# HGRN2 head norm: both scaling multiplications issued one turn later, the first half's product in another tile

## The chip, the core and the metric

The kernel runs on one core of a Trainium2 chip. The metric is the device time of one execution in microseconds; three executions of the kernel before took 1461.38, 1464.78 and 1465.36 us (median 1464.78). A further execution was recorded by the hardware profiler. PE is the matrix engine (PEld its weight loads), DVE the vector engine, ACT the scalar engine, POOL the general engine GpSimd, SP the engine that here only issues DMAs.

## The reference, cut to what matters

The program is one layer of a hybrid trunk on x of 1 x 1024 x 1024: an input projection feeds three mixers (HGRN2 of four heads, attention over dilated windows, RWKV-7), whose outputs are concatenated and projected back; then a gated MLP, a gated embedding and a last norm. The change lies in the end of each HGRN2 head:

```python
_, o = lax.scan(step, s0, (chunks(q), chunks(k), chunks(i_raw.astype(f32)), chunks(log_f)))
o = o.transpose(1, 0, 3, 2, 4).reshape(B_, S_, HG_HEADS, HG_VDIM)
o = o * lax.rsqrt(jnp.mean(o * o, axis=-1, keepdims=True) + NORM_EPS)
o = o.reshape(B_, S_, HG_WIDTH) * gnorm_g.astype(f32) * jax.nn.silu(g_raw.astype(f32))
```

Per head o has 1024 positions x 128 values. Each position is divided by the root of the mean square of its 128 values, then multiplied by a weight and a gate.

## The kernel before, in words

The kernel works in f32 throughout; big matrix products are made of three passes over a split into high and low parts (L130, L132, L134). Its phases in order of time: the input norm and the first projections, RWKV with the other projections as filler, then from about 440 to 620 us the stretch in which the change lies (`phase_mix`, L317 to L328), then the output projection (`phase_out`), the MLP and the rest.

In the stretch four Python generators are issued in turns, and each `yield` ends a turn: A is HGRN2 head 0 and then head 2, B is head 1 and then head 3, C is the window attention (`swa`), F the last input projections (`project_late`, tiles named zp and zst). What a turn issues is not yet the order on the chip: a scheduler, which works with modelled times, places the instructions on each engine's queue when the program is built. The engines then run their queues in that order and wait for each other by semaphores. So moving a `yield` or a line changes the queues only where the scheduler's modelled times come out in another order.

A head (`hgrn_head`) works on positions laid along the 1024 columns of [128, 1024] tiles, which come from one pool of 11 slots (`self.slot`). It goes in these steps:

- f and q are loaded from DRAM (L984, L985, by SP; tile name zl). f is scaled (L987, DVE), k = 1 - f in two halves (L990, tile hk) and q*f (L992, 1024 wide, tile qt).
- Scores in eight levels: products (L1008, L1029, tile hsc), a masked copy into the score tile (L1010, L1031, tile hS), and updates of k (L1032, DVE or POOL in turn), of qt (L1034, DVE) and of the running products of f (L1039, tile hT). ACT copies the next level's keys (L1019, tile ks).
- Two masked copies close the scores (L1045, L1046).
- v is transposed (L1052) and copied to the tile hV (L1053), the keys likewise to hkt (L1058, L1059); the states are chained (L1073, L1080, L1082, tile hst).
- The output: for each half `hf`, PE makes four 128x128 blocks from hS and hV and from qt and hst (L1103, L1105); ACT copies them to the tile ho (L1106). `head_factor` makes the factor of the norm: squares on ACT into the old hkt (L1093), sum on DVE (L1094), mean and epsilon on DVE (L1095), power -1/2 on POOL (L1096, tile hrs). The half 0 uses the first half of hV, the half 1 the second.
- In the next turn the gate is loaded (L1110), the second half's factor is made and both halves of ho are multiplied by the factor, in place (L1114, DVE). After two more turns, of which one is empty, PE transposes the halves (L1121, tile vt), and DVE multiplies by weight and gate (L1122). The result is split for the output projection (`o_split`, `split_x`: ACT L155, then POOL or DVE L157; tiles xh, xl).

Other work that shares the queues here: the split of weights (L106 on ACT, L108 on POOL or DVE), the scaling of the last projections (L306, L475), the copies, sums and scaling of the attention (L1193 is one pass over logits, tile lg; L1210, tile pT; L1225 a small reciprocal; L1233, tile ob), and PE's attention products (L1186 tile swq, L1209 swt, L1222 swo, L189 swd). The PSUM pool mx, with four buffers, serves hsc, zp, vt, hkv, hpo, swt, swo and swd alike, so a late reader of one of these tiles holds up a PE product that needs the next buffer.

Of the kernel before, what the change touches and what calls it, by code (L numbers as in the profile page):

```python
# [14 lines left out]
ALU = mybir.AluOpType  # L15
# [3 lines left out]
P = 128  # L19
T = 1024  # L20
HT = 512
# [58 lines left out]
class Trunk:  # L80
# [896 lines left out]
    def hgrn_head(self, h):  # L977
        nc, mxp, par, spool = self.nc, self.mxp, self.par, self.spool
# [69 lines left out]
        V = self.slot("hV")  # L1048
        for hf in (0, 1):
            pt = mxp.tile([P, HT], F32, tag="mx", name=self.nm("vt"))  # L1050
# [4 lines left out]
        for hf in (0, 1):  # L1055
            pt = mxp.tile([P, HT], F32, tag="mx", name=self.nm("vt"))
# [30 lines left out]
        o3 = o.rearrange("p (c v) -> p c v", v=P)  # L1087
        sq3 = sq.rearrange("p (c v) -> p c v", v=P)
        ss, rs = (spool.tile([P, 8], F32, tag=n, name=self.nm(n)) for n in ("hss", "hrs"))

        def head_factor(hf):
            cs = slice(4 * hf, 4 * hf + 4)
            nc.scalar.activation(sq3[:, cs, :], o3[:, cs, :], AF.Square)  # L1093
            nc.vector.tensor_reduce(ss[:, cs], sq3[:, cs, :], AX.X, ALU.add)  # L1094
            nc.vector.tensor_scalar(ss[:, cs], ss[:, cs], 1.0 / P, EPS, ALU.mult, ALU.add)  # L1095
            nc.gpsimd.tensor_tensor(rs[:, cs], ss[:, cs], self.mhalf[:, :4], ALU.pow)  # L1096
# [12 lines left out]
        yield  # L1109
        oa = self.zload(j0 + 3, self.slot)  # L1110
        head_factor(1)
        for hf in (0, 1):
            oh = o3[:, 4 * hf:4 * hf + 4, :]
            nc.vector.tensor_tensor(oh, oh, rs[:, 4 * hf:4 * hf + 4].unsqueeze(2).broadcast_to([P, 4, P]), ALU.mult)  # L1114
        yield
        yield
        for hf in (0, 1):
            sl = slice((1 - hf) * HT, (2 - hf) * HT)
            pt = mxp.tile([P, HT], F32, tag="mx", name=self.nm("vt"))
            for c in range(4):  # L1120
                nc.tensor.transpose(pt[:, c * P:(c + 1) * P], o3[:, hf * 4 + c, :], self.ident)  # L1121
            nc.vector.scalar_tensor_tensor(oa[:, sl], pt if hf else pt[:, ::-1], par[:, PC_GN + h:PC_GN + h + 1], oa[:, sl], ALU.mult, ALU.mult)  # L1122
        self.o[h] = oa
        self.dump(f"o{h}", oa)
# [754 lines left out]
```

## Time and profile before

| what | value |
|---|---|
| median of three runs | 1464.78 us (1461.38 to 1465.36) |
| profiled execution, its own time | 1464.15 us |
| its span on the core (first to last instruction) | 1462.4 us |
| what lies around the span | 1.75 us |
| PE busy | 1431.1 us (98% of the span) |
| DVE busy | 1099.2 us (75%) |
| ACT, POOL busy | 636.1 us (44%), 447.8 us (31%) |
| granted TensorE clock, mean | 0.994 |
| stretch of the four heads, 490 to 620 us | PE busy 119.90 of 130 us, DVE 102.83 |

In a row of the timeline stand the start in us, the duration in us, the engine, the line, the operation, the tile written and the tiles read, their shapes and the count; in brackets the idle time of that engine just before the row and what ended it. Rows with a count above one are neighbours put together. In the table of windows a number stands beside each engine's busy time in brackets: the count of instructions. Idle time matters where it lies on the engine that the end of the program depends on.

### The profile page before, as it was taken

The numbers are of one execution on the slowest core, as the hardware profiler recorded it, in microseconds if no ns is written. First come the engines' busy times: TensorE is split into PE (matmuls) and PEld (weight loads), VectorE is DVE, ScalarE is ACT, GpSimd is POOL, SyncE is SP. The second block draws the span as 40 slices with busy tenths as digits, with TensorE's granted clock in tenths as the row PEclk, the third lists the DMA queues.
The fourth block names the chain that finished last, engine by engine and source line by source line (L and its number), as shares of the span: only waits on it lengthen the run. The fifth ranks groups of instructions, "written<-read, shape, count | busy, mean of one in ns | idle before, by whom it ended". The sixth has DMA issues, their size and how long they took to land.

```text
span 1462.4 us, 20341 instructions
## 1 busy us (share of the span) xinstructions
PE 1431.1 (98%) x7480; PEld 1178.0 (81%) x7480; DVE 1099.2 (75%) x1672; ACT 636.1 (44%) x1131; POOL 447.8 (31%) x364
## 2 busy tenths in 40 slices
PE   9999999999999999899989999999999999999996
PEld 7888887888877777788878888888888888888885
DVE  7667565674677688638778898888898799777685
ACT  6531443213434565335544344444444444455552
POOL 3331342223321131222144554444554000002342
PEclk9999999999999999999999999999999999999998
DMA  6123021240251320265423333333233883352343
GB/s 220 63 90 105 33 71 58 65 130 30 73 188 51 108 73 30 71 219 204 156 87 105 99 100 108 102 108 106 97 107 111 309 293 95 102 172 58 123 157 116
DMA packets 80020, 167.84 MB, mean 115 GB/s; under 512 B 20081, under 2 KB 22257, under 8 KB 79921
## 3 DMA queue, kind: packets, MB, share of 16 engines
q1 hardware_dynamic: 65568, 145.44, 30.2%
q10 hardware_dynamic: 13408, 17.57, 3.6%
q0 software_dynamic: 944, 3.54, 0.7%
q8 instruction: 59, 0.97, 0.3%
q14 instruction: 41, 0.33, 0.1%
HBM read 120.12 MB, written 46.40 MB: 114 GB/s over the span
## 4 chain that ended last, share of the span: by engine, by line
PE 87%; DVE 4%; issue 3%; ACT 2%; POOL 2%; DMA 2%; SPq 0%; DVEq 0%; ACTq 0%; POOLq 0%
PE bg L1351 16%; PE bv L1351 12%; PE dp L130 8%; PE dp L134 8%; PE dp L132 8%; PE bg L1652 7%; PE bv L1652 7%; PE hsc L1029 1%; PE bv L130 1%; PE bv L132 1%; PE bv L134 1%; PE bg L130 1%; PE bg L134 1%; PE bg L132 1%; PE swq L1186 1%
## 5 line engine op out<-in xcount | busy, mean ns | idle before, releaser
L130 PE MATMUL dp<-xh,whi 128*128 128x512 f32 x544 | 197.5, 408 | 0.8 <-ACT xh L375 0.8
L134 PE MATMUL dp<-xh,wlo 128*128 128x512 f32 x544 | 188.9, 392 | 0.3 <-POOL wlo L108 0.3
L132 PE MATMUL dp<-xl,whi 128*128 128x512 f32 x544 | 188.6, 392 | 0.0
L108 POOL TENSOR_TENSOR wlo<-raw,whi 128x512 fp32r<-128x512 f32 x84 | 138.0, 1662 | 80.9 <-ACT whi L106 80.9
L108 POOL TENSOR_TENSOR wlo<-wraw,whi 128x512 fp32r<-128x512 f32 x63 | 89.2, 1420 | 226.2 <-ACT whi L106 208.2
L1351 PE MATMUL bg<-t,whi 128*128 128x512 f32 x352 | 132.7, 389 | 0.0
L106 ACT CAST whi<-wraw 128x512 fp32r<-128x512 f32 x120 | 72.6, 617 | 129.1 <-PE dp L132 87.1
L130 PEld LDWEIGHTS dp<-xh,whi 128*128 128x128 f32 x544 | 101.6, 189 | 23.6 <-issue 3.5
L134 PEld LDWEIGHTS dp<-xh,wlo 128*128 128x128 f32 x544 | 102.3, 188 | 22.5 <-POOL wlo L108 0.7
L132 PEld LDWEIGHTS dp<-xl,whi 128*128 128x128 f32 x544 | 102.5, 189 | 20.2 <-DVE xl L376 0.5
L108 POOL TENSOR_TENSOR wlo<-s,whi 128x512 fp32r<-128x512 f32 x44 | 65.7, 1492 | 159.1 <-ACT whi L106 159.1
L106 ACT CAST whi<-raw 128x512 fp32r<-128x512 f32 x88 | 52.6, 619 | 100.3 <-PE bv L1351 51.5
L1652 PE MATMUL bg<-t,whi 128*128 128x512 f32 x308 | 94.9, 389 | 0.0
L1652 PE MATMUL bv<-t,whi 128*128 128x512 f32 x308 | 94.8, 389 | 0.0
L106 ACT CAST whi<-s 128x512 fp32r<-128x512 f32 x66 | 38.9, 620 | 120.7 <-PE bg L1351 113.0
L175 POOL TENSOR_TENSOR rst<-rst,mhalf 128x4 f32<-128x4 f32 (+1 forms) x9 | 10.2, 1130 | 222.7 <-DVE rst L173 222.7
L108 DVE TENSOR_TENSOR wlo<-wraw,whi 128x512 fp32r<-128x512 f32 x57 | 47.7, 837 | 40.2 <-ACT whi L106 35.8
L1351 PEld LDWEIGHTS bg<-t,whi 128*128 128x128 f32 x352 | 66.1, 188 | 13.7
L1648 ACT CAST t<-t 128x512 fp32r<-128x512 f32 x77 | 47.8, 622 | 47.9 <-PE bv L1652 33.0
L1652 PEld LDWEIGHTS bv<-t,whi 128*128 128x128 f32 x308 | 57.8, 188 | 12.0
L1652 PEld LDWEIGHTS bg<-t,whi 128*128 128x128 f32 x308 | 57.8, 188 | 11.9
L1351 PE MATMUL bg<-t,wlo 128*128 128x512 f32 x176 | 67.2, 389 | 0.0
(424 smaller groups left out, 3616.6 us busy)
## 6 DMA issues: line engine op xcount, KB each, us to landing
raw<-in_ffn_up_dram SPq DMA_DIRECT2D x44, 512.0 KB, 3.7
wraw<-in_w_in_dram SPq DMA_DIRECT2D x29, 512.0 KB, 3.7
z<-zst SPq DMA_DIRECT2D x18, 512.0 KB, 3.0
gb<-ct SPq DMA_DIRECT2D x33, 256.0 KB, 2.3
t<-gb SPq DMA_DIRECT2D x33, 256.0 KB, 2.8
t<-gt SPq DMA_DIRECT2D x33, 256.0 KB, 2.7
zl<-z SPq DMA_DIRECT2D x16, 512.0 KB, 4.5
wraw<-in_ple_gate_dram SPq DMA_DIRECT2D x16, 512.0 KB, 3.6
```

The costliest lines, as they stand in the source:

```text
L106: nc.scalar.copy(hi, src)
L108: eng.tensor_tensor(lo, src, hi.bitcast(F32), ALU.subtract)
L130: nc.tensor.matmul(ps[hf], wh, xh[hf], start=first, stop=False)
L132: nc.tensor.matmul(ps[hf], wh, xl[hf], start=False, stop=False)
L134: nc.tensor.matmul(ps[hf], wl, xh[hf], start=False, stop=last)
L175: nc.gpsimd.tensor_tensor(r2[:, :n], r[:, :n], self.mhalf[:, :n], ALU.pow)
L1029: nc.tensor.matmul(sc[:, c, :], ks[:, c * P:(c + 1) * P], view(qt, c * P, [2 * n, 64 // n], [HT + n, 2], [1, n]), start=True, stop=True)
L1186: nc.tensor.matmul(pq[h][:, b:b + w], d["q"][hs, qb * P:nk], d["k"][hs, b:b + w], start=True, stop=True)
L1351: nc.tensor.matmul(ps, w[part == 2][:, s], X[k][part == 1], start=start and k == part == 0, stop=k == 3 and part == 2, skip_group_check=no ...
L1648: nc.scalar.copy(xh, x)
L1652: nc.tensor.matmul(ps[m], wt[part == 2][:, m * P:(m + 1) * P], (xh, xl)[part == 1], start=k == part == 0, stop=k == NK - 1 and part == 2)
```

## The change

The two multiplications L1114 move behind one `yield`: they are issued one turn later, where before there was an empty turn. The first half's product is no longer written over ho but into the first half of hV, whose last reader in the program before was the half 0 of the output product. The transposes read the first half from there. The second half is still multiplied in place. The change adds no instruction that computes; hV stays in use until the transposes, and so does its slot.

```diff
@@ -1109,16 +1109,17 @@
         yield
         oa = self.zload(j0 + 3, self.slot)
         head_factor(1)
+        yield
+        normed = [V[:, :HT].rearrange("p (c v) -> p c v", v=P), o3[:, 4:, :]]
         for hf in (0, 1):
-            oh = o3[:, 4 * hf:4 * hf + 4, :]
-            nc.vector.tensor_tensor(oh, oh, rs[:, 4 * hf:4 * hf + 4].unsqueeze(2).broadcast_to([P, 4, P]), ALU.mult)
-        yield
+            cs = slice(4 * hf, 4 * hf + 4)
+            nc.vector.tensor_tensor(normed[hf], o3[:, cs, :], rs[:, cs].unsqueeze(2).broadcast_to([P, 4, P]), ALU.mult)
         yield
         for hf in (0, 1):
             sl = slice((1 - hf) * HT, (2 - hf) * HT)
             pt = mxp.tile([P, HT], F32, tag="mx", name=self.nm("vt"))
             for c in range(4):
-                nc.tensor.transpose(pt[:, c * P:(c + 1) * P], o3[:, hf * 4 + c, :], self.ident)
+                nc.tensor.transpose(pt[:, c * P:(c + 1) * P], normed[hf][:, c, :], self.ident)
             nc.vector.scalar_tensor_tensor(oa[:, sl], pt if hf else pt[:, ::-1], par[:, PC_GN + h:PC_GN + h + 1], oa[:, sl], ALU.mult, ALU.mult)
```

The lines behind it move by one: L1114 becomes L1116, L1122 becomes L1123, and so on.

In the queues the change moves nothing on POOL and SP, and a handful of rows on the others. Two places matter. The first is DVE at the end of head 0, where head 2 begins. The names: qt_4617 is head 2's q*f (L992); xl are splits for the output projection; zp and zst are a projection; hS and qt_3996 belong to head 1, zl_4446 is head 0's gate. Before:

```order
L992 TENSOR_TENSOR qt_4617<-zl_4550,zl_4548 128x1024
L157 TENSOR_TENSOR xl_4706<-ob_3827,xh_4705 128x512
L157 TENSOR_TENSOR xl_4710<-oc_1628,xh_4709 128x512
L306 TENSOR_TENSOR zp_4477<-zp_4477,rstd 128x512
L1031 COPY_PREDICATED hS_4036<-cmask,hsc_4506 128x512
L1034 TENSOR_TENSOR qt_3996<-qt_3996,hT_4038 128x2x8x32
L157 TENSOR_TENSOR xl_4712<-oc_3237,xh_4711 128x512
L1122 SCALAR_TENSOR_TENSOR zl_4446<-vt_4536,par,zl_4446 128x512
L475 TENSOR_TENSOR zst_4475<-zst_4475,zp_4477 128x512
L1122 SCALAR_TENSOR_TENSOR zl_4446<-vt_4542,par,zl_4446 128x512
L1031 COPY_PREDICATED hS_4036<-cmask,hsc_4552 128x512
L1034 TENSOR_TENSOR qt_3996<-qt_3996,hT_4038 128x2x4x64
```

And the end of the same piece with the change, which begins with the two L157 in the place of L992:

```order
L1123 SCALAR_TENSOR_TENSOR zl_4446<-vt_4542,par,zl_4446 128x512
L1031 COPY_PREDICATED hS_4036<-cmask,hsc_4552 128x512
L1034 TENSOR_TENSOR qt_3996<-qt_3996,hT_4038 128x2x4x64
L992 TENSOR_TENSOR qt_4617<-zl_4550,zl_4548 128x1024
L1045 COPY_PREDICATED hS_4036<-cmask,hS_4036 128x512
L157 TENSOR_TENSOR xl_4698<-zl_4446,xh_4697 128x512
```

L992 has moved behind eleven rows, to the place ahead of L1045. On SP the loads stand in the same order, but head 2's load of q now carries the wait that head 1's load of v, the next in the queue, had before, since the slots are given out otherwise.

The second place is DVE at the end of head 1. ho_4771, hss_4772 and hrs_4773 are head 1's; hS_4647 and hT_4649 are head 2's scores; zl_4907 is head 3's f; lg, swq and sden are the attention's. Before:

```order
L1193 ISA lg_4859,sden_4602<-swq_4853,swmask 128x512
L1193 ISA sden_4602 128x1
L1114 TENSOR_TENSOR ho_4771<-ho_4771,hrs_4773 128x512
L1031 COPY_PREDICATED hS_4647<-cmask,hsc_4841 128x512
L1034 TENSOR_TENSOR qt_4617<-qt_4617,hT_4649 128x2x64x4
L1032 TENSOR_TENSOR hk_4614<-hk_4614,hT_4649 128x2x32x8
L987 TENSOR_SCALAR zl_4907<-zl_4907,olb,lb 128x1024
L1225 RECIPROCAL sden_4602<-sden_4602 128x8
L1031 COPY_PREDICATED hS_4647<-cmask,hsc_4880 128x512
```

With the change:

```order
L1194 ISA lg_4859,sden_4602<-swq_4853,swmask 128x512
L1194 ISA sden_4602 128x1
L1031 COPY_PREDICATED hS_4647<-cmask,hsc_4839 128x512
L1034 TENSOR_TENSOR qt_4617<-qt_4617,hT_4649 128x2x64x4
L1116 TENSOR_TENSOR ho_4771<-ho_4771,hrs_4773 128x512
L1032 TENSOR_TENSOR hk_4614<-hk_4614,hT_4649 128x2x32x8
L1031 COPY_PREDICATED hS_4647<-cmask,hsc_4880 128x512
```

The second half's multiplication now stands behind one level's masked copy and its update of qt; L987 moves eleven rows down, ahead of its reader L990, with one L1032 between the two, and L1225 still further. On PE the same place had two attention products ahead of the score product hsc_4880 and now has one; the transposes follow the score product as before.

In the queues of heads 0, 2 and 3 the multiplications themselves stand where they stood.

## The prediction

> **What bounds the kernel now.** I read the page first: busy times, then the chain that ended last.
>
> ```profile
> span 1462.4 us, 20341 instructions
> PE 1431.1 (98%) x7480; PEld 1178.0 (81%) x7480; DVE 1099.2 (75%) x1672; ACT 636.1 (44%) x1131; POOL 447.8 (31%) x364
> ...
> PE 87%; DVE 4%; issue 3%; ACT 2%; POOL 2%; DMA 2%; SPq 0%; DVEq 0%; ACTq 0%; POOLq 0%
> ```
>
> PE is the bound: 1431.1 of 1462.4 us. An edit on DVE counts only where PE stands idle for DVE, or comes to. So I went to the windows around the two places where the queues differ (first number the width; then PE, PEld, DVE, ACT and POOL):
>
> ```profile
> 512.00:524.00 12.00, 11.79 (x101) 9.67 (x96) 11.77 (x16) 7.13 (x13) 5.38 (x4) 1.00 0.06 23
> 524.00:540.00 16.00, 16.00 (x112) 13.12 (x114) 11.87 (x34) 12.70 (x31) 6.01 (x6) 1.00 0.34 108
> 540.00:557.00 17.00, 14.46 (x112) 10.89 (x110) 16.44 (x32) 7.92 (x19) 3.84 (x5) 1.00 0.21 71
> ...
> 490.00:620.00 130.00, 119.90 (x945) 99.06 (x942) 102.83 (x196) 69.39 (x138) 33.64 (x30) 0.99 0.22 75
> ```
>
> From 512 to 524 us DVE is as full (11.77 of 12) as PE; from 524 to 540 PE never rests; from 540 to 557 DVE is full (16.44 of 17) and PE idles 2.54 us. What PE waits for in the whole stretch of the heads, 490 to 620 us (total, times, longest):
>
> ```profile
> PE hsc L1029 <- DVE qt L1034: 4.6, 4, 2.1
> PE vt L1121 <- DVE ho L1114: 1.5, 1, 1.5
> ```
>
> With some small ones it idles 10.1 us there (130 less 119.90), which caps any gain here. About 0.3% of this time, 4.4 us, is what a measurement can tell from no change; the cap is over that, the sums below are not.
>
> **The change part by part.** *The multiplications themselves.* There are eight, at 692 ns by the group's row, and eight after, with the same shape, so nothing is added to DVE's work.
>
> ```profile
> L1114 DVE TENSOR_TENSOR ho<-ho,hrs x8: 690/692/1533, 502.8 to 613.1; 128x512 f32<-128x512 f32 x8
> L1122 DVEq EVENT_SEMAPHORE  x4: 21/21/21, 511.8 to 613.1; - x4
> ```
>
> The first half's product into hV must also wait until PE has read hV. That wait is already over whenever the factor exists, since the factor is made from that product. What it costs is an added semaphore row on DVE: 0.02 us by the second row, three heads at most, 0.06 us; I take 0.05.
>
> *Head 2's q\*f (L992) eleven rows later.* The rows of DVE, with the ACT and POOL rows beside them:
>
> ```profile
> 507.69 0.80 DVE L987 TENSOR_SCALAR zl<-zl,olb,lb 128x1024 f32<-128x1024 f32 x1
> ...
> 509.20 1.22 DVE L992 TENSOR_TENSOR qt<-zl,zl 128x1024 f32<-128x1024 f32 x1
> ...
> 510.21 1.31 ACT L155 CAST xh<-oc 128x512 fp32r<-128x512 f32 x2 [0.74 <-PE zp L134]
> ...
> 510.94 0.68 DVE L157 TENSOR_TENSOR xl<-oc,xh 128x512 fp32r<-128x512 f32 x1
> ```
>
> Before, L992 filled a hole. The second xl behind it needs a cast on ACT that starts at 510.21, after a wait for PE, and two take 1.31 us, so it can't start before about 510.87 whatever DVE does. If L992 leaves, DVE stands idle for most of its 1.22 us and nothing behind comes earlier. Eleven rows on, it lands here:
>
> ```profile
> 516.82 0.67 DVE L1034 TENSOR_TENSOR qt<-qt,hT 128x512 f32<-128x512 f32 x1
> 517.23 1.41 POOL L157 TENSOR_TENSOR xl<-zl,xh 128x512 fp32r<-128x512 f32 x1 [10.01 <-ACT xh L155]
> ...
> 517.41 1.83 DVE L1045 COPY_PREDICATED hS<-cmask,hS 128x512 f32<-128x512 uint8 x1
> ...
> 519.06 1.30 POOL L108 TENSOR_TENSOR wlo<-wraw,whi 128x512 fp32r<-128x512 f32 x1 [0.42 <-ACT whi L106]
> ...
> 519.14 1.77 DVE L157 TENSOR_TENSOR xl<-zl,xh 128x512 fp32r<-128x512 f32 x1
> ...
> 568.03 0.72 DVE L1045 COPY_PREDICATED hS<-cmask,hS 128x512 f32<-128x512 uint8 x1
> ```
>
> L1045 alone takes 0.72 us (568.03); at 517.41 it took 1.83. POOL's row ended at 518.64, and L1045 at 519.24, 0.60 later: it stood still while POOL worked, and only then ran. The xl at 519.14 did the same behind POOL's L108 (520.36 to 520.91). So DVE's chain here is full and partly stalled, and it ends on PE:
>
> ```profile
> 523.13 0.67 DVE L1233 TENSOR_TENSOR ob<-ob,swd 128x512 f32<-128x512 f32 x1
> ...
> 523.95 1.06 PE L1058 MATMUL vt<-cst,hk 128*128 128x128 f32 x8 [0.21 <-DVE ob L1233]
> ```
>
> PE waits 0.21 us for L1233, which frees a PSUM buffer. There is no slack: what DVE loses between 517.4 and 523.8, PE loses at 523.95, and PE is full up to 540.
>
> With the change L992 starts at 517.41 and, having two inputs in SBUF like the xl, stands until POOL is done at 518.64; with its 1.14 (1.22 less the overlap of neighbouring rows) it ends about 519.78. Then come L1045 and the xl. If L1045 stands for POOL's L108 up to 520.4, it ends at 521.0; the xl is then free, and ends at 521.65, against 520.83 where the next row began before: +0.8 us. If the stalls stay as they are, the whole 1.14 comes on top. Bounds: nothing, where L992 isn't stalled and uses up the time in which L1045 stood; and +2.9, where each handover goes to POOL (rival 1). I take +1.0, nearest to the two rows that stalled.
>
> The Trainium skill ("SBUF — State Buffer", section "SBUF: two separate sides") says that an operation of DVE with two SBUF inputs and a GpSimd operation that reads SBUF exclude each other, and whoever starts first keeps the ports for the whole instruction. By that L992 would be held and would then hold POOL's L108. The two stalled rows agree with its first half; whether POOL then pushes back is rival 1.
>
> *The loads.* On SP, head 2's load of q takes over the wait that the next load in the queue had.
>
> ```profile
> 499.81 1.27 SPq L503 DMA_DIRECT2D zl<-z  x3
> ...
> DMA to landing us min/median/max: 3.1/4.2/5.9
> ```
>
> All three loads were issued within 1.27 us, so that wait was over by 500.66. At the longest landing, 5.9 us, q is there by 507, ten us before its new reader. Cost nil; without that cover, the delay of L992 would come on top.
>
> *Head 1's second half behind a masked copy and an update of qt.*
>
> ```profile
> 543.13 0.69 DVE L1193 CUSTOM_DVE_ANT_0 lg<-swq,swmask 128x512 f32<-128x512 f32 x1
> ...
> 544.34 0.69 DVE L1114 TENSOR_TENSOR ho<-ho,hrs 128x512 f32<-128x512 f32 x1 [0.52 <-POOL hrs L1096]
> 544.95 0.72 DVE L1031 COPY_PREDICATED hS<-cmask,hsc 128x512 f32<-128x512 uint8 x1
> 545.56 0.68 DVE L1034 TENSOR_TENSOR qt<-qt,hT 128x512 f32<-128x512 f32 x1
> ...
> 546.39 1.13 PE L1029 MATMUL hsc<-qt,ks 128*128 128x128 f32 x8 [0.72 <-DVE qt L1034]
> ...
> 554.04 1.13 PE L1029 MATMUL hsc<-qt,ks 128*128 128x128 f32 x8 [0.35 <-DVE qt L1034]
> 555.00 1.95 PE L1008 MATMUL hsc<-zl,hk 128*128 128x128 f32 x16
> ```
>
> DVE waited 0.52 us for the factor with a masked copy behind it whose product was long there. In the new order the copy starts at 543.8, qt is done about 545.0 instead of 546.2, and PE starts the score product about 545.1; one attention product now stands behind it, so nothing runs dry. PE wins most of the 0.72. The second wait, 0.35, goes too, as that product stands earlier. But the next one needs head 3's k:
>
> ```profile
> 553.81 0.76 DVE L990 TENSOR_SCALAR hk<-zl 128x512 f32<-128x512 f32 x2
> ```
>
> DVE's work up to the end of L990 (554.57) loses the wait of 0.52 and L1225 (0.12 as the rows step), and gains one L1032 that came later before (0.60): 554.53. So L1008 can start at 554.6 instead of 555.00: a gain of 0.4 us. That is what is late next. Bounds: 0, if POOL stalls another row here, and 0.72 + 0.35 = 1.07.
>
> *The other heads.* Heads 0, 2 and 3 keep their multiplications where they were. The last head shows what the edit might have shortened:
>
> ```profile
> 613.07 0.69 DVE L1114 TENSOR_TENSOR ho<-ho,hrs 128x512 f32<-128x512 f32 x1 [1.12 <-POOL hrs L1096]
> ...
> 613.91 1.06 PE L1121 MATMUL vt<-cst,ho 128*128 128x128 f32 x8 [1.54 <-DVE ho L1114]
> ```
>
> There the half 1 comes first on DVE and the half 0 last, and PE's queue has the half 0 first, before as after. So the 1.54 us stay.
>
> The sum: +1.0 - 0.4 + 0.05 = +0.65 us, on the profiled execution's own time of 1464.15 (span 1462.4 and 1.75 around): 1464.8 us. The median of the three runs is 1464.78, 0.6 over the profiled execution, and the lowest 1461.38, 2.8 under it; so this forecast is "no change".
>
> **The rivals.**
>
> *1. Slower: POOL and DVE hold each other up in turn.* Place: DVE and POOL from 517 to 526 us. L992 ends at 519.78, then POOL's L108 goes first (1.30, to 521.08), L1045 ends at 521.7, POOL's next split comes between again (1.5 us), and L1233 ends near 526.7 instead of 523.8: +2.9, less 0.4 and plus 0.05, gives 1466.7 us. It decides if POOL gets its turn at each of the two handovers. For it: POOL has four rows in 5.38 us of that window. Against it: the second of these splits waits for its own cast. Chance 0.2.
>
> *2. A little faster: L992 costs nothing.* If L992 runs beside POOL, and L1045 behind it is stalled less, the two rows take the time of the one. Then only -0.4 and 0.05 are left: 1463.8 us. For it: the L1034 at 516.82 kept its 0.67 us although POOL's row began before its end. Chance 0.2.
>
> *3. Faster: the last head's transposes no longer wait.* With the halves in two tiles, PE could start on one half while DVE works on the other; the 1.54 us of the last head would go: 1464.15 + 0.65 - 1.5 = 1463.3 us. Against: the queue has the late half first. Chance 0.05.
>
> *4. The change doesn't do what it says.* In three heads of four this is so already, since the scheduler had put the multiplications where their factor is ready. It is part of the forecast.
>
> **How the numbers follow.** The forecast has 0.5, rivals 1 to 3 have 0.2, 0.2 and 0.05; 0.05 is left for something that I don't see, such as shifted DMAs behind the stretch. All cases lie between 1463.3 and 1466.7 on the profiled execution; the three runs lay from 2.8 under to 1.2 over it, but their median varies less. I put 2 us below the lowest case and 0.3 above the highest: 1461.3 to 1467.0. The threshold of 4.4 us is reached by none of the cases, whether counted from 1464.15 or from the median. So: within 0.3% 0.92, faster by more 0.04 and slower by more 0.04, from the unseen rest and the spread of the runs.
>
> **What would show it right or wrong.** In the profile after: L992 near 517.4 with a duration over 1.22, idle DVE near 509.5, PE's L1058 about 1 us later with a wait of 1 us or more for DVE (under 0.3: rival 2; over 2: rival 1); near 545 the masked copy ahead of the multiplication and PE's wait there under 0.3; L1121 of the last head with its 1.5 us unchanged. I would be wrong if PE's idle time between 490 and 620 us changed by more than 3 us, or if the time moved with that idle time unchanged.

## The result, and the profile after

The kernel before took 1463.24 us (median of 8 runs, 1461.38 to 1465.36), the changed one 1467.93 us (8 runs, 1465.41 to 1469.87): ratio 1.0033, 95% interval 1.0023 to 1.0044, about +4.7 us, where +0.65 us and a time from 1461.3 to 1467.0 us were forecast. The profiled execution after took 1469.87 us (span 1468.1 and 1.8 around), 5.7 over the profiled one of before. The page after:

```profile
span 1468.1 us, 20345 instructions
PE 1433.5 (98%) x7480; PEld 1177.7 (80%) x7480; DVE 1101.9 (75%) x1672; ACT 636.3 (43%) x1131; POOL 448.2 (31%) x364
```

The same 7480 products keep PE busy 2.4 us longer, and the span has grown by 5.7. So both waits and the products themselves have to be looked at.

**End of head 0.** DVE, POOL and PE in the timeline after (start, duration; in brackets the idle time before and what ended it):

```profile
516.17 1.42 POOL L157 TENSOR_TENSOR xl<-zl,xh 128x512 fp32r<-128x512 f32 x1 [10.00 <-ACT xh L155]
516.37 2.31 DVE L992 TENSOR_TENSOR qt<-zl,zl 128x1024 f32<-128x1024 f32 x1
...
518.00 1.82 POOL L108 TENSOR_TENSOR wlo<-wraw,whi 128x512 fp32r<-128x512 f32 x1 [0.41 <-ACT whi L106]
...
518.60 1.83 DVE L1045 COPY_PREDICATED hS<-cmask,hS 128x512 f32<-128x512 uint8 x1
...
520.27 2.95 POOL L157 TENSOR_TENSOR xl<-oc,xh 128x512 fp32r<-128x512 f32 x2 [0.44 <-ACT xh L155]
520.32 1.77 DVE L157 TENSOR_TENSOR xl<-zl,xh 128x512 fp32r<-128x512 f32 x1
...
522.01 1.79 DVE L1046 COPY_PREDICATED hS<-cmask,few 128x512 f32<-128x512 uint8 x1
...
524.91 0.67 DVE L1234 TENSOR_TENSOR ob<-ob,swd 128x512 f32<-128x512 f32 x1
...
525.73 1.94 PE L1058 MATMUL vt<-cst,hk 128*128 128x128 f32 x8 [3.05 <-DVE ob L1234]
...
527.46 3.62 PE L1008 MATMUL hsc<-zl,hk 128*128 128x128 f32 x16
```

L992 takes 2.31 us in place of 1.22, and at every handover DVE and POOL stand for each other: L992 until POOL's split ends at 517.59, POOL's L108 until L992 ends at 518.68, L1045 until L108 ends at 519.82. PE's wait for L1234 has become 3.05 us (0.21 before). And then the products behind it are slow. In the windows after (width, busy time of PE, PEld, DVE, ACT and POOL, then the granted clock, 1.00 being full speed):

```profile
524.00:526.00 2.00, 0.27 (x2) 0.30 (x3) 2.00 (x4) 1.56 (x3) 0.00 (x0) 0.68 0.00 0
526.00:528.00 2.00, 2.00 (x11) 2.00 (x10) 0.60 (x5) 1.06 (x2) 0.00 (x0) 0.50 0.93 285
528.00:530.00 2.00, 2.00 (x11) 2.00 (x11) 0.59 (x1) 1.99 (x6) 0.00 (x0) 0.50 0.32 117
530.00:532.00 2.00, 2.00 (x14) 2.00 (x12) 0.89 (x2) 0.69 (x2) 0.84 (x1) 0.62 0.00 0
```

And PE's L1008 of before, with the clock at 1.00:

```profile
524.85 1.95 PE L1008 MATMUL hsc<-zl,hk 128*128 128x128 f32 x16
```

The clock is halved from about 524.7 to 531.5 us (by the shares of the first and the last window), and L1058 and L1008 take 1.94 and 3.62 us in place of 1.06 and 1.95. The same 122 products that follow from L1058 on (525.73 to 547.71 us, and 523.95 to 543.14 before) keep PE busy 20.59 us in place of 17.82. A wait of 3 us has cost PE nearly as much again.

**End of head 1.** DVE and PE after:

```profile
548.30 0.74 DVE L1031 COPY_PREDICATED hS<-cmask,hsc 128x512 f32<-128x512 uint8 x1
...
549.11 1.12 PE L1187 MATMUL swq<-zl,zl 64*128 64x512 f32 x2
549.52 0.68 DVE L1116 TENSOR_TENSOR ho<-ho,hrs 128x512 f32<-128x512 f32 x1
...
550.16 1.16 PE L1029 MATMUL hsc<-qt,ks 128*128 128x128 f32 x8
...
552.12 1.34 PE L1187 MATMUL swq<-zl,zl 64*128 64x512 f32 x6
...
555.24 1.22 DVE L157 TENSOR_TENSOR xl<-zl,xh 128x512 fp32r<-128x512 f32 x1
556.12 2.26 PE L1187 MATMUL swq<-zl,zl 64*128 64x512 f32 x4
556.38 0.81 DVE L1194 CUSTOM_DVE_ANT_0 lg<-swq,swmask 128x640 f32<-128x640 f32 x1
...
557.25 0.29 PEld L1187 LDWEIGHTS swq<-zl,zl 64*128 64x128 f32 x2 [0.84 <-DVE sden L1194]
```

The masked copy runs ahead of the multiplication, and PE's score product at 550.16 waits for nothing. But the attention products have changed. Before:

```profile
544.54 1.13 PE L1186 MATMUL swq<-zl,zl 64*128 64x512 f32 x4
...
548.33 0.49 PE L1186 MATMUL swq<-zl,zl 64*128 64x128 f32 x4
...
551.80 1.89 PE L1186 MATMUL swq<-zl,zl 64*128 64x512 f32 x8
```

Each uses 64 of PE's 128 rows. Two heads' products of 512 columns, one behind the other, took 1.13 us together (x4), and after, one alone takes 1.12 (x2): as a pair they run side by side. After, one pair is parted by the score product and the transposes (1.12 + 1.34 against 1.13 + 0.49), another by time: its second half must wait until the second logit pass (L1194) frees its buffer, and an xl of 1.22 us has come between the two passes (2.26, and 0.70 more for its 256 wide rest, against 1.89). This place of the xl is a third change in DVE's queue, beside the two shown ahead of the prediction: before, it stood behind both passes (551.99 us, 0.69 long).

**The sum.** From the transposes of head 0 to head 3's score product that waits longest for qt (595.00 before, 600.56 after): first all products, then the rows of the attention's tile swq alone (the products L1186 and L1187 with their weight loads and the DVE rows that read them; busy time of PE, PEld and DVE), of before:

```profile
513.58:595.00 81.42, 74.77 (x580) 59.67 (x579) 70.55 (x140) 47.29 (x101) 23.01 (x20) 1.00 0.16 53
```

```profile
513.58:595.00 81.42, 14.33 (x48) 5.47 (x48) 11.72 (x16) 1.00 0.16 53
```

and of after:

```profile
512.53:600.56 88.03, 79.34 (x580) 62.61 (x579) 74.02 (x141) 47.70 (x101) 24.70 (x20) 0.96 0.15 49
```

```profile
512.53:600.56 88.03, 16.24 (x48) 5.58 (x48) 11.76 (x16) 0.96 0.15 49
```

The stretch is 6.61 us longer. PE's idle time went from 6.65 to 8.69: 2.84 more at L1058, 0.80 less elsewhere, nearly all of it at the end of head 1 (1.25 to 0.46). Its busy time grew by 4.57: 1.91 in the attention products, the remaining 2.66 by the half clock (2.77 in the 122 products behind the wait, 0.11 less in overlaps elsewhere). The last head's transposes wait 1.45 us (1.54 before).

### The profile page after: what moved, and what is told of

Read it like the earlier page. It is cut to its first block, busy times and chain, and to the rows that moved or that the text cites. A ratio compares the mean times of both kernels' runs of the same rounds, so it can differ in the third digit from the quotient of the medians.

```text
span 1468.1 us, 20345 instructions
## 1 busy us (share of the span) xinstructions
PE 1433.5 (98%) x7480; PEld 1177.7 (80%) x7480; DVE 1101.9 (75%) x1672; ACT 636.3 (43%) x1131; POOL 448.2 (31%) x364
## 4 chain that ended last, share of the span: by engine, by line
PE 85%; DVE 5%; issue 3%; ACT 3%; POOL 1%; DMA 1%; SPq 0%; DVEq 0%; ACTq 0%; POOLq 0%
PE bg L1352 16%; PE bv L1352 12%; PE dp L130 7%; PE dp L134 7%; PE dp L132 7%; PE bg L1653 7%; PE bv L1653 7%; PE hsc L1029 2%; PE bv L130 1%; PE bv L134 1%; PE bv L132 1%; PE swq L1187 1%; PE bg L130 1%; PE bg L134 1%; PE bg L132 1%
## 5 line engine op out<-in xcount | busy, mean ns | idle before, releaser
L108 POOL TENSOR_TENSOR wlo<-raw,whi 128x512 fp32r<-128x512 f32 x84 | 138.0, 1662 | 80.8 <-ACT whi L106 80.8
L108 POOL TENSOR_TENSOR wlo<-wraw,whi 128x512 fp32r<-128x512 f32 x63 | 88.6, 1410 | 227.8 <-ACT whi L106 209.2
L108 POOL TENSOR_TENSOR wlo<-s,whi 128x512 fp32r<-128x512 f32 x44 | 65.4, 1487 | 159.4 <-ACT whi L106 159.4
L108 DVE TENSOR_TENSOR wlo<-wraw,whi 128x512 fp32r<-128x512 f32 x57 | 48.3, 847 | 40.1 <-ACT whi L106 35.7
```

The source lines that it names most:

```text
L108: eng.tensor_tensor(lo, src, hi.bitcast(F32), ALU.subtract)
```

## The experiments

The theory from these rows: L992's new place makes DVE and POOL stand for each other, PE waits 2.84 us more and falls to half clock; the later turn of the multiplications saves a wait and parts pairs of attention products. Rivals: the prediction's own reading (small and mostly hidden terms); that idle time alone counts, and not the clock; that the order of DVE at the end of head 1 costs, and not the pairs. The median of a kernel before serves the runs beside it: 1461.74 us for the first four, 1462.75 for the next four, 1462.88 for the last two.

Medians scatter, and the clock also falls elsewhere in some profiles (in that of before to a mean of 0.83 from 495 to 505 us, in that of after it stays at 1.00 there). So beside them stands, for each profile, the stretch of the sum above, between the same two products, with PE's busy and idle time and the attention products (us):

| kernel | stretch | PE busy | PE idle | attention products |
|---|---|---|---|---|
| before | 81.42 | 74.77 | 6.65 | 14.33 |
| after | 88.03 | 79.34 | 8.69 | 16.24 |
| other tile alone | 85.87 | 76.39 | 9.48 | 14.33 |
| later turn alone | 82.43 | 76.58 | 5.85 | 16.24 |
| after, L992 of head 2 on POOL | 82.43 | 76.55 | 5.88 | 16.24 |
| after, 24 transposes repeated | 86.03 | 78.63 | 7.40 | 15.55 |
| after, 16 transposes repeated | 86.09 | 77.77 | 8.32 | 15.55 |
| before, L992 of head 3 on POOL | 83.58 | 75.51 | 8.07 | 13.21 |
| before, one pair parted | 81.75 | 75.07 | 6.68 | 14.65 |
| later turn, that pair kept | 82.32 | 75.53 | 6.79 | 15.11 |

**1. The other tile alone.** The first half's product goes to hV, and the turn stays.

```diff
+        normed = [V[:, :HT].rearrange("p (c v) -> p c v", v=P), o3[:, 4:, :]]
         for hf in (0, 1):
-            oh = o3[:, 4 * hf:4 * hf + 4, :]
-            nc.vector.tensor_tensor(oh, oh, rs...
+            cs = slice(4 * hf, 4 * hf + 4)
+            nc.vector.tensor_tensor(normed[hf], o3[:, cs, :], rs...
         yield
         yield
```

> The other tile alone: the first half's product goes to hV, but the multiplications keep their old turn. In the queues only L992 of head 2 moves late, as in the change; head 1's end is as before. Theory (two costs at head 0's end: DVE and POOL hold each other up, 2.9 us at PE's wait ahead of L1058, and PE then runs at half clock for some 5 us, 2 to 2.7 us more; head 1's end costs about 1 us): slower than before by 4 to 5.5 us, L992 about 2.3 us long, PE's wait for L1233 about 3 us, granted clock 0.5 behind it. Rival 1 (the late multiplications cost the time): within 1 us of before. Rival 2 (waits alone count, the clock does not): slower by 2.5 to 3.2 us.

Measured: 1466.46 us (12 runs, 1464.2 to 1471.94), ratio 1.0033, interval 1.0020 to 1.0046. PE and two windows of its profile:

```profile
525.44 1.06 PE L1058 MATMUL vt<-cst,hk 128*128 128x128 f32 x8 [3.05 <-DVE ob L1234]
526.34 3.36 PE L1008 MATMUL hsc<-zl,hk 128*128 128x128 f32 x16
```

```profile
526.00:528.00 2.00, 2.00 (x14) 2.00 (x13) 0.31 (x4) 1.80 (x2) 0.00 (x0) 0.65 0.85 308
528.00:530.00 2.00, 2.00 (x11) 2.00 (x11) 0.92 (x2) 1.93 (x7) 0.21 (x1) 0.50 0.16 53
```

The same wait of 3.05 us and a half clock behind it, here for about 3.4 us. The attention products keep their 14.33. The median is 4.7 us over the kernel before, within the theory's 4 to 5.5, and the stretch 4.45 longer: this part alone makes up most of the loss.

**2. The later turn alone.** The multiplications move, both in place.

```diff
-        for hf in (0, 1):
-            oh = o3[:, 4 * hf:4 * hf + 4, :]
-            nc.vector.tensor_tensor(oh, oh, rs...
         yield
+        normed = [o3[:, :4, :], o3[:, 4:, :]]
+        for hf in (0, 1):
+            cs = slice(4 * hf, 4 * hf + 4)
+            nc.vector.tensor_tensor(normed[hf], o3[:, cs, :], rs...
         yield
```

> The later turn alone: the multiplications move behind one yield, both halves still in place in ho. L992 of head 2 stays early; the end of head 1 is as in the change. Theory: slower than before by 0.3 to 1.5 us (0.8 us won ahead of the score product, 1.7 us lost where a pair of attention products is parted and a split comes between two logit passes). Rival 1: slower by 4 to 5 us. Rival 3 (the prediction's own reading of this place): faster by 0.4 us.

Measured: 1463.61 us (12 runs, 1461.17 to 1466.93), ratio 1.0013, interval 1.0002 to 1.0025 (+1.9 us, a little over the theory's 0.3 to 1.5; +1.01 in the stretch, within it). The table splits it: PE idles 0.80 us less, as in the whole change, and works 1.81 longer, 1.91 of it in the attention products. The prediction's gain of 0.4 us at this place falls.

**3. The change, with head 2's q\*f on POOL.**

```diff
-        nc.vector.tensor_tensor(qt, q, f, ALU.mult)
+        (nc.gpsimd if h == 2 else nc.vector).tensor_tensor(qt, q, f, ALU.mult)
```

> The change, with head 2's q*f (L992) computed on POOL in place of DVE; nothing else moves in the queues. POOL is idle from 507 to 516 us there. Theory: the wait ahead of L1058 is back under 0.5 us, the clock stays full, what is left is head 1's end: slower than before by 0.3 to 1.5 us, so 3.5 to 4.5 us under the change. Rival 4 (hV's longer life and the slots cost the time, not the place of L992 on DVE): as slow as the change, 4 to 5 us over before.

Measured: 1464.5 us (12 runs, 1461.37 to 1466.73), ratio 1.0015, interval 1.0003 to 1.0026. PE's wait is gone, and L1008 runs at full clock:

```profile
523.86 1.06 PE L1058 MATMUL vt<-cst,hk 128*128 128x128 f32 x8 [0.25 <-DVE ob L1234]
524.76 1.95 PE L1008 MATMUL hsc<-zl,hk 128*128 128x128 f32 x16
```

With L992 off DVE, the change costs what the later turn alone costs (82.43 us in both stretches). So the loss at the end of head 0 hangs on that one instruction's place, and in the stretch the other tile has no cost of its own. The median misses, though: 2.8 us over the kernel before, where 0.3 to 1.5 were expected and rival 4 had 4 to 5; its interval (0.4 to 3.8 us) leaves open whether anything outside the stretch is lost.

**4 and 5. The change, with PE's hole filled.** Head 1's second transposes of v are repeated in the same buffer, 6 times (24 more) in one kernel and 4 times (16 more) in the other.

```diff
             for c in range(4):
                 nc.tensor.transpose(pt[:, c * P:(c + 1) * P], vc[...], self.ident)
+            for _ in range(4 if h == 1 and hf else 0):
+                for c in range(4):
+                    nc.tensor.transpose(pt[:, c * P:(c + 1) * P], vc[...], self.ident)
```

> The change, with 24 of head 1's value transposes repeated on PE (same values into the same place), about 2.6 us of products in the hole of 3.05 us ahead of L1058. Theory: PE is not idle over 0.6 us there, the granted clock stays 1.0, L1058 takes about 1.1 us again in place of 1.94 and L1008 about 1.95 in place of 3.62; the copies on ACT come in another order, which gives about 1 us back; 1 to 2.5 us under the change. Rival 2 (the clock has no part): as slow as the change or slower.

> The change, with PE's hole at the end of head 0 part filled: head 1's second transposes of v are repeated 4 times in the same buffer (16 transposes, some 1.8 us by the rate of the 24 in the run before this one, which took about 2.6), instead of 6 times. The results are the same. Theory (half clock): PE's wait ahead of the key transposes falls from 3.05 to about 1.3 us, the clock stays at 1.00 from 524 to 534 us, and the time is 2 to 2.8 us under the changed kernel's on the same chip. Rival (what the idle time costs is the idle time alone, and the slow rows are a matter of the records): the same time as the changed kernel, within 1 us.

Measured: with 24, 1468.97 us (6 runs, 1468.59 to 1470.7), ratio 1.0049 (1.0031 to 1.0066). With 16, 1468.08 us (5 runs, 1467.77 to 1471.19), ratio 1.0041 (1.0028 to 1.0055), beside the changed kernel's own run (6, below): 1469.29. PE with 24:

```profile
526.73 1.06 PE L1060 MATMUL vt<-cst,hk 128*128 128x128 f32 x8 [0.45 <-DVE ob L1236]
...
530.01 1.16 PE L1008 MATMUL hsc<-zl,hk 128*128 128x128 f32 x8 [1.32 <-ACT hV L1055]
```

With 16, PE and one of the windows:

```profile
525.66 1.06 PE L1061 MATMUL vt<-cst,hk 128*128 128x128 f32 x8 [1.33 <-DVE ob L1237]
```

```profile
526.00:528.00 2.00, 1.62 (x15) 1.43 (x13) 0.88 (x6) 1.97 (x5) 1.70 (x2) 1.00 0.81 277
```

In both the clock stays at 1.00 from 524 to 534 us, and the 122 products that follow keep PE busy 17.27 us in place of 20.59 in after: the slow rows did come from the idle time. (0.69 of these 3.32 us lie in attention products that came together in these kernels; the other 2.63 are the half clock's.) The stretch is 1.9 to 2.0 us shorter than after's, the order of what was expected. The whole time is a miss: with 16 it was 1.2 us under the changed kernel's, where 2 to 2.8 were expected, and with 24 it was 7.2 over the kernel before, not under the 4.7 and 6.5 of the changed kernel's two sets of runs. By the time alone the rival of 4, that the clock has no part, would stand; the rows speak against it. Part of the reason is in the row at 530.01: ACT's copies came later in these kernels, and PE stands another 1.3 us for one of them. In the profile with 24, another 1.7 us lies ahead of the stretch:

```profile
428.64 2.05 DVE L987 TENSOR_SCALAR zl<-zl,olb,lb 128x1024 f32<-128x1024 f32 x1
...
431.48 1.54 PE L1029 MATMUL hsc<-qt,ks 128*128 128x128 f32 x8 [1.91 <-DVE hS L1010]
```

There L987 started together with a POOL row of 1.49 us (L1032, 428.65) and took 2.05 us, where it takes 0.80 in after; the masked copy behind it came late, and PE waited 1.91 us in place of 0.21. Whether every execution has this isn't shown. The rest was not found, and ranges that overlap leave it open.

**6. The changed kernel again.** No edit.

> The changed kernel as it is, once more, beside the three that run with it, so that they have it and the kernel before as their measure on one chip. Theory: about +4.7 us against the kernel before, as in its first eight runs (2.8 of it PE's longer wait ahead of L1058, some 2.5 the half clock behind it, 1 at the end of head 1, less what other waits take up). Rival (the earlier 4.7 us was a matter of which executions kept the clock in the holes near 495 us): under +2.

Measured: 1469.29 us (5 runs, 1468.26 to 1471.54), ratio 1.0043, interval 1.0031 to 1.0055. Its profile repeats the wait (3.06 us) and the half clock (0.61, 0.50, 0.50 in the windows from 526 to 532 us). The loss is there again, and not smaller.

**7. The kernel before, with the attention's loops exchanged.** Meant to part the pairs.

```diff
-        for b in range(0, nk, HT):
-            w = min(HT, nk - b)
-            for h, hs in enumerate(self.HEADS):
+        for h, hs in enumerate(self.HEADS):
+            for b in range(0, nk, HT):
+                w = min(HT, nk - b)
```

> The kernel before, with the two loops of the attention's products exchanged, so that each head's blocks of columns come together and the products of the two heads (64 rows each) no longer stand in turns. The work is the same. Theory (two 64-row products in a row run side by side, a pair of 512 columns in 1.13 us where one alone takes 1.12): each of up to eight parted pairs costs about 1.1 us on PE; PE is full for most of that stretch, so +4 to +9 us. Rival (that the change parts one such pair is nothing, and only the waits for DVE count): within 1.5 us of the kernel before.

Measured: 1459.83 us (12 runs, 1458.2 to 1463.47), ratio 0.9981, interval 0.9972 to 0.9991: faster, by about 2.8 us. Both expectations miss. The row at the place of the pair:

```profile
541.49 1.34 PE L1186 MATMUL swq<-zl,zl 64*128 64x512 f32 x6
```

Products of 512, 128 and 512 columns take 1.34 us: with only 64-row products between them, the two heads still run side by side. So the exchange didn't part the 512 wide pair there; only the 128 wide one came apart, for 0.21 us (1.34 + 0.49 against 1.13 + 0.49). Ahead of the stretch it put pairs together that the order of before had parted. The attention products alone, before:

```profile
418.00:493.50 75.50, 12.48 (x48) 4.63 (x48) 11.43 (x16) 1.00 0.26 90
```

and with the loops exchanged:

```profile
418.00:493.50 75.50, 11.11 (x48) 4.47 (x48) 11.59 (x16) 1.00 0.28 100
```

1.37 us less for the same 48 rows, and the output products that follow start at 493.33 in place of 494.76. So pairs count here as well, in the other direction; the rest of the 2.8 us wasn't traced (PE also waits 0.60 us less from 418 us to these output products, 1.64 in place of 2.24). This version is faster than both kernels.

**8. The kernel before, with head 3's q\*f on POOL.** The edit of 3 with `h == 3`.

> The kernel before, with head 3's q*f (L992, 1.22 us on DVE at 554.5) put on POOL, which is idle there from 552.4 to 557.7. Theory (at the end of head 1 DVE is the bound, 16.44 of 17 us): PE's waits between 554 and 570 shrink, and the time falls by 0.3 to 1.2 us. Rival (a POOL operation of that width locks DVE out for its whole length of some 2.5 us, as POOL's rows at 517 to 520 did): DVE's two-input rows beside it stretch, and the time is 0 to 1.5 us longer.

Measured: 1465.7 us (11 runs, 1463.33 to 1468.78), ratio 1.0018, interval 1.0008 to 1.0028: slower. POOL, DVE and PE:

```profile
550.88 2.36 POOL L992 TENSOR_TENSOR qt<-zl,zl 128x1024 f32<-128x1024 f32 x1
...
550.97 2.81 DVE L157 TENSOR_TENSOR xl<-zl,xh 128x512 fp32r<-128x512 f32 x1
...
555.13 1.34 PE L1029 MATMUL hsc<-qt,ks 128*128 128x128 f32 x8 [2.48 <-DVE qt L1034]
```

A split of 0.69 us takes 2.81 beside POOL's L992, 0.5 us past its end at 553.24, and PE waits 2.48 us in place of 0.35. The rival holds, above its range (+2.9 us, where 0 to 1.5 were given). Here too the clock falls behind the wait (0.50 from 556 to 558 us); the attention products happen to take 1.12 us less, which hides part of the loss.

**9. The kernel before, with one pair parted.**

```diff
             for h, hs in enumerate(self.HEADS):
-                nc.tensor.matmul(pq[h][:, b:b + w], ...)
+                with self.tc.issue_after(self.turned) if (d["p"], qb, h, b) == (1, 4, 1, 0) else nullcontext():
+                    nc.tensor.matmul(pq[h][:, b:b + w], ...)
```

Here `self.turned` is the head's last transpose (L1121), which this product is now ordered behind.

> The kernel before, with one pair of attention products parted at the end of head 1: the second head's 512 wide product is issued behind the transposes, as it comes to stand with the change. The work is the same, and the multiplications stay where they are. Theory (what the later turn costs is this pair and what follows from it): PE's rows show two 512 wide products alone, 1.12 us each, in place of one pair of 1.13, and the time is 0.5 to 2 us over the kernel before, like the later turn alone (1.9). Rival (PE's waits for DVE there absorb it, and the later turn's cost lies in the order of DVE): within 0.5 us of the kernel before.

Measured: 1463.05 us (12 runs, 1460.02 to 1467.04), ratio 1.0001, interval 0.9991 to 1.0011. The rival's number, but not for its reason:

```profile
543.26 1.34 PE L1186 MATMUL swq<-zl,zl 64*128 64x512 f32 x4
...
547.04 1.34 PE L1186 MATMUL swq<-zl,zl 64*128 64x512 f32 x4
...
562.60 1.77 PE L1186 MATMUL swq<-zl,zl 64*128 64x512 f32 x8
```

The parted pair costs 2.68 us in place of 1.62, as expected. But the scheduler, with one edge more, also joined another pair at 562.60, of which one half stood alone in before (1.12 at 561.70, then 1.77), and parted a third at 551 us (1.55 and 0.70 in place of 1.89). In all the attention products take 0.32 us more, and the stretch is 0.33 longer: PE's idle time is the same (6.68 to 6.65), so nothing absorbed it.

**10. The later turn, with that pair kept.** Both of its products issued behind the transposes.

> The later turn alone, in place, with that pair of attention products kept together: both are issued behind head 1's transposes. The work is the same. Theory: the pair takes 1.13 us again, the gain of the earlier score product (0.7 to 0.8 us) stays, and of the later turn's +1.9 us some 0.2 to 1 are left, since the logits now come later. Rival (the cost lies in the order of DVE, where a split stands between the two logit passes): +1.5 to +2.5 us as without it.

Measured: 1464.31 us (12 runs, 1461.7 to 1467.2), ratio 1.0011, interval 1.0001 to 1.0022. That pair is together, and the next one is parted again:

```profile
545.75 1.35 PE L1193 MATMUL swq<-zl,zl 64*128 64x512 f32 x8
...
549.76 1.12 PE L1193 MATMUL swq<-zl,zl 64*128 64x512 f32 x2
...
551.11 1.12 PE L1193 MATMUL swq<-zl,zl 64*128 64x512 f32 x4 [0.23 <-DVE sden L1200]
```

The attention products take 0.78 us more than before, and the stretch is 0.90 longer. The median is 1.4 us over the kernel before, between the two ranges (0.2 to 1 and 1.5 to 2.5), and its interval covers both; the stretch agrees with the theory's size. But not with its reason: the saved waits are gone (6.79 us idle, 6.65 before and 5.85 with the later turn alone), and the time goes to the pairs. The order of DVE seems to act through them, since the second half of the parted pair waits for a logit pass (L1200). A kernel with the later turn and every pair kept was not made.

## Why the prediction was wrong

- **L992's move, +1.0 us: the size failed, and a term was missing.** The place, the stall of L992 for POOL and the missing slack at L1058 came as described. The step that failed is the choice between the bounds: "I take +1.0, nearest to the two rows that stalled". At each handover POOL went first, so rival 1 came true, to within 0.06 us of its price (2.84 for 2.9). That it came so near is in part luck: its working had two handovers, while the trace after has L1045, the xl and L1046 all stand for POOL, and a row that stood for POOL before and no longer does (DVE's L108, 0.67 us in place of 1.15). The argument against it, that POOL's second split waits for its own cast, failed by 0.05 us: that split started at 520.27, DVE's xl at 520.32. Experiment 1 shows it with the tile alone, and experiment 3 takes it away by moving L992. The quoted rows of before spoke for it more than a chance of 0.2 says: both of DVE's long rows stood to the end of POOL's instruction.
- **The half clock was in no case.** The sum priced a wait at its own length, and put at nothing what an idle PE does to the products behind it. Behind 3.05 us of idle PE they cost another 2.66 us (1.6 in experiment 1). Filling the hole keeps the clock full (experiments 4 and 5). The hint was there: in before's own profile the clock falls to half near 495 us (0.66 on the mean of 495 to 500), behind two waits of PE (0.69 and 1.09 us).
- **Head 1's end, -0.4 us: the wait went, the products grew.** The waits saved are 0.80 us, against bounds of 0 to 1.07. The step "one attention product now stands behind it, so nothing runs dry" failed: that product was half of a pair. The order shown before the result has it ("had two attention products ahead of the score product hsc_4880 and now has one"), and the prediction read there only whether PE had work, not what the work costs apart. Of the 1.91 us, 0.84 is the pair parted by order, the rest the pair parted by the later logit pass. Experiments 2, 9 and 10 agree with this in their rows, and experiment 7 in the other direction; no kernel with the later turn and all pairs kept closes the case.
- **Right:** the semaphores and loads cost nothing that shows; DVE idles near 509.5 us (0.22 and 0.66 us around a split), and what stands behind comes less than 0.1 us earlier, counted from head 0's transposes; the last head's wait is unchanged.
- **The signs.** The sign "over 2: rival 1" named the larger cause at once. But the last sign was blunt: PE's idle time in the heads' stretch grew by only 2 us, under the 3 that were announced, while the time grew by over 6 there. Busy time is not a fixed quantity.

The sum by what the runs show: +2.84 (wait at L1058), +2.66 (half clock), -0.80 (waits at head 1), +1.91 (pairs) = +6.61 us in this execution, of which the span keeps 5.7, since before's profile lost about 1 us to its half clock near 495 us. The median difference is 4.7 us, interval 3.4 to 6.4; the second set of runs gave 6.5.

## What to carry to other kernels

When an engine's queue is full and stalls against another engine, price one more instruction there by the chain of handovers and not by its own length, and ask what the resulting hole does to the clock of PE. When an order moves on PE, compare not only what waits but which neighbours stay neighbours: here two half-height products cost as much as one (1.13 us) only while nothing of full height, and no wait for a buffer, came between them. Compare busy time and idle time apart, between two fixed products, since the whole time scatters by more than such terms.

## What the runs showed of the hardware

- The clock fell to half with waits of PE of 3.05 us (after, and the tile alone) and 2.48 us (experiment 8); two waits of 1.33 us with 2.0 us between them (experiment 5) left it full. In the profile after it fell about 2.0 us after PE went idle (522.68 to 524.7), within the wait, and stayed down for 6.8 us; with the tile alone it fell about 1.2 us after PE had started again (525.44 to 526.6), and stayed down for about 3.4. Whether such waits cost the clock differs between executions: before's profile has it at 0.66 from 495 to 500 us behind waits of 0.69 and 1.09 us, that of experiment 9 at 1.00 behind the same two. The Trainium skill ("TensorE: Matmul & The Clock Gate", "Part 1: The HAM clock gate (the "warmup" mystery)") has the clock fall after an idle window of about 3.4 us that runs free, and come back after a busy one. The lengths of 3.4 and 6.8 agree with one and two such windows; a rule that the window must be idle from end to end doesn't, since no wait here was as long as that.
- A masked copy stalls against POOL like a two-input operation: L1045 took 1.83 us and L1046 1.79 in place of 0.72 and 0.73. The Trainium skill ("SBUF — State Buffer", "SBUF: two separate sides") names the rule for two SBUF inputs; these rows agree if the mask counts as one.
- Two products of 64 rows ran side by side even with a third of 64 rows between them (1.34 us for 512, 128 and 512 columns), but not with a product of 128 rows between them (1.12 and 1.34).
